# Experts' weights as two neighbouring rows per partition, all 1024 columns at once, a load's slot blocks in turn

## The chip, the cores and the metric

The kernel runs on one core of one Trainium2 chip. The metric is the device time of one execution in microseconds (us), the median over runs. The engines are TensorE (PE; its weight loads are listed apart as PEld), VectorE (DVE), ScalarE (ACT), GpSimd (POOL) and SyncE (SP), which here mainly issues DMAs.

## What is computed

The program is two transformer blocks, one after the other, all in float32. The first has four kinds of attention on 512 tokens. The second has two layers, each with attention, a convolution and a mixture of 16 experts in which every expert chooses its tokens. The change is in the experts of the second block and in the scale and shift that stand ahead of them:

```python
def ec_moe(h, w_router, w_gate, w_up, w_down):       # h: modulate(x, shift, scale)
    cap = EC_CAPACITY * n_tok // N_EXPERTS
    aff = softmax(einsum('bnd,de->bne', h, w_router))
    g, idx = lax.top_k(swapaxes(aff, 1, 2), cap)     # each expert takes cap tokens
    xs = vmap(lambda hb, ib: hb[ib])(h, idx)
    hid = silu(einsum('becd,edf->becf', xs, w_gate)) * einsum('becd,edf->becf', xs, w_up)
    ye = einsum('becf,efd->becd', hid, w_down) * g[..., None]
    return vmap(lambda yb, ib: zeros((n_tok, d)).at[ib.reshape(-1)].add(yb.reshape(-1, d)))(ye, idx)
```

An expert's gate, up and down matrices are 1024 x 1024 each, 4 MB. Layer 0 runs the experts on the latent tokens (64 per expert) and, with the same weights, on the context tokens (32 per expert). Layer 1 runs them on the latent tokens alone.

## The kernel before

`moe` (from L1103) goes through groups of experts: four groups of four in layer 0 (`two` is true), eight groups of two in layer 1. A group has blocks of up to 128 columns of gathered tokens. In layer 0 these are ctx (four experts of 32 tokens), lat0 and lat1 (two experts of 64 tokens each); in layer 1 it is one latent block. `gather` (L1150) fetches a block's token rows `r` with an indirect DMA on POOL's queue, transposes them on TensorE by pieces of 128 (`ptm`), and writes `xT` with scale and shift taken from the columns `modc`.

`wload` (L1126) brings 1 MB of one expert's matrix into a slot `w`: 512 contraction rows by 512 columns, where partition p holds rows p, 128 + p, 256 + p and 384 + p, so each run in memory is 512 columns, 2 KB. There are 14 slots in layer 0 and 18 in layer 1, filled in program order by SP's queue (the last few of the first turn of layer 1 by POOL's). The loads of the last group's down product are smaller in layer 1: 256 columns, runs of 1 KB.

`product` (L1190) multiplies one matrix, 512 columns at a time, with one PSUM bank (`pm`, six of them) for each block. Tokens are the stationary operand: experts of one block lie side by side in TensorE's columns (`tile_position`), four 32-wide or two 64-wide. In the order called `every`, each of the eight contraction steps k goes through ctx, lat0 and lat1 before the next k. Within a group, the loop at L1213 does gate and up for columns 0 to 511, then silu (ACT) into a tile `ty`, the product with up (DVE), and the transposes into `hid`; then the same for columns 512 to 1023. Down follows, again by two column halves. In all groups but the last of layer 0, `down` writes the weighted rows `ys`, and POOL adds them to `accc` (ctx) and `accl` (latent) in memory by indirect DMAs (L1334), one expert at a time. In layer 1, `spread` adds them instead by matmuls with a one-hot matrix `sel`. `r`, `ys` and, in layer 1, `xT` and `hid` are tiles of one pool, shown as `q`, of seven buffers.

`adaln` (L415) computes scale, shift and gates of a layer into `mr`, writes them to memory (`mod`), reads them back as `mraw` (L435), and transposes that to columns `modc`. It runs beside the attention; the second layer's begins by a MEMSET of its `mr` on POOL (L417) and four reads into it on SP (L419). The tile scheduler sets the order of instructions on an engine where the code's own order leaves it open; `pin` fixes some.

## Time and profile before

| | us |
|---|---|
| median of 3 runs | 2866.74 (2864.62 to 2875.64) |
| profiled execution, own time | 2861.59 |
| its span in the trace | 2859.8 |
| TensorE busy | 2483.4 (87%) |
| VectorE / ScalarE / POOL busy | 1228.3 (43%) / 802.2 (28%) / 504.6 (18%) |
| DMA | 612.94 MB, mean 214 GB/s |

The profiled execution lies 5.2 us below the median. TensorE's share of busy time is an average over stages with different limits, so the stages have to be read one by one. The experts of layer 0 take the stretch from 1300 to about 1937 us, those of layer 1 the stretch from about 2338 us to nearly the end. Matmuls in float32 are recorded twice each.

### The profile page before, as it was taken

How to read it: one execution, taken by the hardware profiler on the slowest of the kernel's cores; microseconds unless marked ns; L12 is line 12 of the kernel's file. 1: busy time of each engine (PE TensorE's matmuls, PEld its weight loads, DVE VectorE, ACT ScalarE, POOL GpSimd, SP SyncE). 2: the span in 40 equal slices, each digit the busy share in tenths (PEclk: the TensorE clock that was granted, in tenths of full speed). 3: DMA queues.
4: the chain of work that ended last, by engine and by line, in shares of the span. 5: the costliest groups of instructions: out<-in, count | busy, mean ns of one | idle time of the engine just before them, and what ended most of it. 6: DMA issues, size and time to landing. Idle time of an engine off the chain costs nothing.

```text
span 2859.8 us, 36332 instructions
## 1 busy us (share of the span) xinstructions
PE 2483.4 (87%) x14703; PEld 1412.3 (49%) x14703; DVE 1228.3 (43%) x2361; ACT 802.2 (28%) x1522; POOL 504.6 (18%) x389
## 2 busy tenths in 40 slices
PE   7988898998998878968999999995898869877886
PEld 5755676665687566753222222234677733323233
DVE  5423554335649968762010101028678641212113
ACT  3362323353335436521000000004247320000001
POOL 2111312012223332331010101004223320000001
PEclk9999999999999988988999999997999979999998
DMA  5364553346433141169999998963221479999997
GB/s 183 104 195 126 163 146 110 123 131 186 143 112 132 55 152 36 45 232 326 342 354 340 330 355 297 340 234 104 66 66 37 147 267 387 387 387 387 387 387 272
DMA packets 354191, 612.94 MB, mean 214 GB/s; under 512 B 37585, under 2 KB 110823, under 8 KB 354023
## 3 DMA queue, kind: packets, MB, share of 16 engines
q1 hardware_dynamic: 344214, 576.71, 58.4%
q0 software_dynamic: 5824, 20.45, 2.3%
q10 hardware_dynamic: 3984, 13.45, 1.2%
q8 instruction: 116, 1.90, 0.3%
q14 instruction: 53, 0.43, 0.0%
HBM read 581.88 MB, written 28.67 MB: 213 GB/s over the span
## 4 chain that ended last, share of the span: by engine, by line
PE 39%; DVE 11%; DMA 9%; issue 7%; ACT 3%; POOL 2%; SPq 0%; DVEq 0%; POOLq 0%; ACTq 0%
PE pm L151 24%; PE pj L151 6%; DMA w<-in_w_up_dram 5%; PE pa L151 5%; DMA w<-in_w_down_dram 3%; DVE acc L850 2%; PE pt L151 2%; PE pt L160 1%; DVE wl L331 1%; PE ptm L160 1%; POOL lnst L249 1%; DVE s L245 1%; ACT P L456 1%; DVE Q L1609 0%; DVE ng L453 0%
## 5 line engine op out<-in xcount | busy, mean ns | idle before, releaser
L151 PE MATMUL pm<-w,q 128*64 128x512 f32 (+1 forms) x1600 | 368.9, 583 | 56.2 <-DMA w<-in_w_up_dram 23.0
L151 PE MATMUL pm<-w,xT 128*64 128x512 f32 (+1 forms) x2048 | 389.4, 607 | 0.4 <-DVE xT L1168 0.3
L151 PEld LDWEIGHTS pm<-w,q 128*64 128x64 f32 x1600 | 124.8, 137 | 276.5 <-issue 174.7
L329 ACT ACTIVATE wh<-w 128x1024 fp32r<-128x1024 f32 (+2 forms) x154 | 161.0, 1050 | 303.4 <-PE pj L151 103.4
L1223 DVE TENSOR_TENSOR ty<-pm,ty 128x512 f32<-128x512 f32 x40 | 27.6, 691 | 502.9 <-PE pm L151 502.9
L151 PEld LDWEIGHTS pm<-w,xT 128*64 128x64 f32 (+1 forms) x2048 | 90.5, 123 | 281.1 <-issue 264.7
L151 PE MATMUL pj<-hTh,wh 128*128 128x512 f32 x512 | 214.4, 420 | 12.2 <-ACT ty L301 6.4
L331 POOL TENSOR_TENSOR wl<-w,wh 128x1024 fp32r<-128x1024 f32 (+1 forms) x57 | 142.4, 2500 | 436.6 <-ACT wh L329 403.9
L151 PE MATMUL pm<-w,hid 128*64 128x512 f32 (+1 forms) x1024 | 210.7, 604 | 0.0
L151 PE MATMUL pj<-hTl,wh 128*128 128x512 f32 x512 | 207.7, 406 | 0.0
L151 PE MATMUL pj<-hTh,wl 128*128 128x512 f32 x512 | 205.1, 404 | 0.0
L331 DVE TENSOR_TENSOR wl<-w,wh 128x1024 fp32r<-128x1024 f32 (+2 forms) x97 | 136.3, 1405 | 104.0 <-ACT wh L329 103.6
L160 PE MATMUL pt<-ident,P 128*128 128x128 f32 x712 | 120.5, 289 | 11.2 <-DVE mx L133 3.1
L151 PE MATMUL pa<-wh,hTh 128*128 128x512 f32 x256 | 106.2, 416 | 23.2 <-DVE ty L948 15.1
L151 PEld LDWEIGHTS pm<-w,hid 128*64 128x64 f32 (+1 forms) x1024 | 47.1, 122 | 154.6 <-issue 152.2
L151 PEld LDWEIGHTS pj<-hTh,wh 128*128 128x128 f32 x512 | 100.2, 196 | 38.9 <-issue 8.1
L1219 ACT ACTIVATE ty<-pm 128x512 f32<-128x512 f32 x40 | 23.9, 597 | 314.6 <-PE pm L151 314.6
L151 PEld LDWEIGHTS pj<-hTl,wh 128*128 128x128 f32 x512 | 99.8, 195 | 24.1 <-issue 3.9
L151 PEld LDWEIGHTS pj<-hTh,wl 128*128 128x128 f32 x512 | 98.7, 193 | 24.4 <-issue 2.2
L135 DVE TENSOR_SCALAR P<-P,rc 128x256 f32<-128x256 f32 (+6 forms) x176 | 107.8, 635 | 4.4
L453 DVE TENSOR_REDUCE ng<-pa 128x1 f32<-128x513 f32 (+5 forms) x124 | 93.3, 756 | 36.9 <-PE pa L151 35.0
L151 PE MATMUL pa<-wh,hTl 128*128 128x512 f32 x256 | 104.4, 412 | 1.1 <-DVE hTl L370 1.1
(441 smaller groups left out, 4332.7 us busy)
## 6 DMA issues: line engine op xcount, KB each, us to landing
w<-in_w_gate_dram SPq DMA_DIRECT2D x128, 1024.0 KB
w<-in_w_up_dram SPq DMA_DIRECT2D x127, 1024.0 KB
w<-in_w_down_dram SPq DMA_DIRECT2D x118, 1024.0 KB
w<-in_w_mod_dram SPq DMA_DIRECT2D x96, 512.0 KB
w<-in_w_in_dram SPq DMA_DIRECT2D x94, 512.0 KB
w<-in_w_out_dram SPq DMA_DIRECT2D x40, 512.0 KB
w<-in_w_down_dram SPq DMA_DIRECT2D x16, 512.0 KB
z<-q ACTq DMA_DIRECT2D x8, 512.0 KB
```

What stands on the lines that cost most here:

```text
L135: (G if eng == "g" else V).tensor_scalar(o, i, scale, None, op0=OP.mult)
L151: return T.matmul(o, l, r, start=start, stop=stop_, skip_group_check=True, **kw)
L160: T.transpose(o, i, ident[: i.shape[0], : i.shape[0]])
L245: pin(V.bn_stats(s6[:, c, :], x[:, c * w:c * w + w]))
L249: pin(G.tensor_tensor(out=rs, in0=ve, in1=mhalf[:, :n], op=OP.pow))
L329: A.activation(hi, w, AF.Copy)
L331: (lo_eng or (G if lot[0] % 3 == 0 else V)).tensor_tensor(out=lo, in0=w, in1=hi.bitcast(F32), op=OP.subtract)
L453: V.tensor_reduce(ng, S_[:, :, lo:hi], axis=AX, op=OP.max, negate=True)
L456: A.activation(P[:, i, lo:hi], S_[:, i, lo:hi], AF.Exp, bias=ng[:, i:i + 1], accum_out=su[:, i:i + 1])
L850: V.scalar_tensor_tensor(acc[:, c, :n], glu[:, c, tap:tap + n], w, acc[:, c, :n], op0=OP.mult, op1=OP.add)
L1219: A.activation(x, g, AF.Silu)
L1223: V.tensor_tensor(out=gs[bi], in0=u, in1=gs[bi], op=OP.mult)
```

## The change

Three things change together.

First, the layout of a load. `wwide` brings 512 rows by all 1024 columns in halves: partition p holds rows 4p + m and 4p + m + 1 of a 512-row half, whole and next to each other in memory, so that one run is 8 KB. A load is still 1 MB, and a matrix still four loads (j = 0 to 3) per expert. The contraction rows are thus permuted, and what multiplies them has to follow: transposes of gathered rows and of the gate/up result read every fourth column (`wide_rows`), and scale and shift come from a new table `modw`. For that, `adaln` reads two small pieces of `mod` back into `mr`, and adds eight transposes of four columns, a copy and two additions for each layer. The last group's down product keeps `wload` and its layout.

Second, the order of the products. `wide` does both column halves of all blocks with all six `pm` banks; for each load index j, it runs the latent blocks and then ctx, each with two contraction steps and two column halves. In the first gate of layer 0 the ctx block goes ahead for three of the four loads. Silu, the product with up and the transposes into `hid` come after both halves. In layer 0 the silu result is in a buffer of the pool `q` (`t4`) in place of `ty`.

Third, down of all groups but the last is one `wide` product, after which `down` and `spread` run for both halves.

```diff
--- before.py
+++ after.py
@@ -401,6 +401,7 @@
     z_d = [dr.tile([S, D], F32, name=f"z{l}") for l in range(NL)]
     mod_d = [dr.tile([2, 6 * D], F32, name=f"mod{l}") for l in range(NL)]
     modc = [con.tile([128, 96], F32, name=f"modc{l}") for l in range(NL)]
+    modw = [con.tile([128, 8, 4], F32, name=f"modw{l}") for l in range(NL)]
     cT = con.tile([128, 8, 32], F32, name="cT")
 
     def cond():
@@ -440,6 +441,20 @@
             for sc in (1, 4):
                 s0 = 48 * c + 8 * sc
                 V.tensor_scalar(modc[l][:, s0:s0 + 8], modc[l][:, s0:s0 + 8], 1.0, None, op0=OP.add)
+
+        mrow = mr[0:4, 0:8, :].rearrange("p a b -> p (a b)")
+        for c in range(2):
+            nc.sync.dma_start(mrow[2 * c:2 * c + 2, :], mod_d[l][c, 3 * D:5 * D].rearrange("(a d) -> a d", a=2))
+        p = pj()
+        for k in range(8):
+            tr(p[:, 4 * k:4 * k + 4], wide_rows(mrow, k))
+        V.tensor_copy(modw[l].rearrange("p k c -> p (k c)"), p[:, :32])
+        for c in range(2):
+            V.tensor_scalar(modw[l][:, :, 2 * c + 1], modw[l][:, :, 2 * c + 1], 1.0, None, op0=OP.add)
+
+    def wide_rows(x, k):
+
+        return x[:, 512 * (k // 4):512 * (k // 4) + 512].rearrange("p (j m) -> p m j", m=4)[:, k % 4, :]
 
     def mc(l, c, chunk, k):
         o_ = 48 * c + 8 * chunk + k
@@ -1121,16 +1136,27 @@
         def pm():
             return psm.tile([128, 512], F32, tag="m", name="pm", bufs=6)
 
-        def wload(src, e, c0, n, kh):
+        def wslot():
             turn[0] = (turn[0] + 1) % len(order_)
             pool = order_[turn[0]]
-            w = pool.tile([128, 4, 512], F32, tag="w", name="w", bufs=slots[id(pool)])
+            return pool.tile([128, 2048], F32, tag="w", name="w", bufs=slots[id(pool)])
+
+        def wload(src, e, c0, n, kh):
+
+            w = wslot().rearrange("p (k c) -> p k c", k=4)[:, :, :n]
+            loads[0] += 1
+            nc.sync.dma_start(w, src[l, e, 512 * kh:512 * kh + 512, c0:c0 + n].rearrange("(k p) c -> p k c", p=128))
+            return w
+
+        def wwide(src, e, j):
+
+            w = wslot().rearrange("p (k c) -> p k c", k=2)
 
             late = len(order_) - LATE[l] <= loads[0] < len(order_)
             loads[0] += 1
-            w = w[:, :, :n]
-            pin((nc.gpsimd if late else nc.sync).dma_start(w, src[l, e, 512 * kh:512 * kh + 512, c0:c0 + n].rearrange(
-                "(k p) c -> p k c", p=128)), late)
+            m = 2 * (j % 2)
+            pin((nc.gpsimd if late else nc.sync).dma_start(
+                w, src[l, e].rearrange("(h p m) c -> p h m c", h=2, m=4)[:, j // 2, m:m + 2, :]), late)
             return w
 
         gms = {}
@@ -1158,10 +1184,11 @@
             for kk in range(2):
                 p = ptm()
                 for k in range(4):
-                    tr(p[:, 128 * k:128 * k + 128], r[:, 512 * kk + 128 * k:512 * kk + 128 * k + 128])
+                    tr(p[:, 128 * k:128 * k + 128], wide_rows(r, 4 * kk + k))
                 for k in range(4):
                     k_ = 4 * kk + k
-                    o, i_, g, b = xT[:, k_, :], p[:, 128 * k:128 * k + 128], mc(l, s["c"], 4, k_), mc(l, s["c"], 3, k_)
+                    b, g = (modw[l][:, k_, 2 * s["c"] + j:2 * s["c"] + j + 1] for j in range(2))
+                    o, i_ = xT[:, k_, :], p[:, 128 * k:128 * k + 128]
                     if k % 2:
                         A.activation(o, i_, AF.Identity, bias=b, scale=g)
                     else:
@@ -1205,26 +1232,52 @@
                                    k == 0, k == 7, tile_position=(0, c0))
                 return outs
 
+            lats = [b for b, x in enumerate(blocks) if x[2] is lat]
+            rest_ = [b for b, x in enumerate(blocks) if x[2] is not lat]
+
+            def wide(src, lhs, early=False):
+
+                ws = {(e, j): wwide(src, e, j) for j in range(4) for e in exps}
+                outs = {}
+                for b in (rest_ + lats if early else lats + rest_):
+                    outs[b] = pm(), pm()
+                steps = [(b, j) for j in range(4) for b in lats + rest_]
+                if early:
+                    first = [(b, j) for j in range(3) for b in rest_]
+                    steps = first + [x for x in steps if x not in first]
+                for b, j in steps:
+                    for k in (2 * j, 2 * j + 1):
+                        for h in range(2):
+                            for e, c0, m in blocks[b][1]:
+                                mm(outs[b][h][c0:c0 + m, :], lhs[b][:, k, c0:c0 + m],
+                                   ws[e, j][:, k % 2, 512 * h:512 * h + 512], k == 0, k == 7, tile_position=(0, c0))
+                return outs
+
             all_k = range(8)
             every = [(list(range(len(blocks))), all_k)]
             one_by_one = [([b], all_k) for b in range(len(blocks))]
             hid = [mB.tile([128, 8, 128], F32, tag=f"hid{j}", name="hid", bufs=1) if two else
                    row4().rearrange("p (a b) -> p a b", b=128) for j in range(len(blocks))]
-            for half in range(2):
-                order = one_by_one if i == 0 and half == 0 else every
-                gp = product(a["w_gate_2"], (512 * half, 512), [b[0] for b in blocks], order)
-                gs = []
-                for g in gp:
-                    x = half_tile()
-                    A.activation(x, g, AF.Silu)
-                    gs.append(x)
-                up = product(a["w_up_2"], (512 * half, 512), [b[0] for b in blocks], order)
-                for bi, u in enumerate(up):
-                    V.tensor_tensor(out=gs[bi], in0=u, in1=gs[bi], op=OP.mult)
+            xTs = [b[0] for b in blocks]
+            gp = wide(a["w_gate_2"], xTs, two and i == 0)
+            gs = {}
+            for b in gp:
+                gs[b] = t4() if two else None
+                for h in range(2):
+                    x = gs[b][:, h, :] if two else half_tile()
+                    A.activation(x, gp[b][h], AF.Silu)
+                    gp[b] = gp[b][:h] + (x,) + gp[b][h + 1:]
+            up = wide(a["w_up_2"], xTs)
+            for b in up:
+                for h in range(2):
+                    x = gp[b][h]
+                    V.tensor_tensor(out=x, in0=up[b][h], in1=x, op=OP.mult)
                     p = ptm()
                     for k in range(4):
-                        tr(p[:, 128 * k:128 * k + 128], gs[bi][:, 128 * k:128 * k + 128])
-                    copy(hid[bi][:, 4 * half:4 * half + 4, :].rearrange("p a b -> p (a b)"), p)
+
+                        tr(p[:, 128 * k:128 * k + 128], x[:, 128 * k:128 * k + 128] if final else
+                           x.rearrange("p (j m) -> p m j", m=4)[:, k, :])
+                    copy(hid[b][:, 4 * h:4 * h + 4, :].rearrange("p a b -> p (a b)"), p)
 
             if i == 0:
                 late_rows()
@@ -1309,6 +1362,8 @@
                     self.seen.add(nm)
 
             waiting = None
+            if not final:
+                dw = wide(a["w_down_2"], hid)
             for c, n in ((0, 256), (256, 256), (512, 256), (768, 256)) if final and not two else ((0, 512), (512, 512)):
                 x = Columns(c, n)
                 if final and two:
@@ -1317,7 +1372,7 @@
                         lambda dp: x.down(1, dp), lambda dp: x.spread(0), ([2], range(4, 6)), lambda dp: x.spread(1),
                         ([2], range(6, 8)), lambda dp: x.down(2, dp), lambda dp: x.spread(2)])
                     continue
-                dp = product(a["w_down_2"], (c, n), hid, one_by_one if final else every)
+                dp = product(a["w_down_2"], (c, n), hid, one_by_one) if final else {b: dw[b][c // 512] for b in dw}
                 for bi in range(len(blocks)):
                     x.down(bi, dp)
                 if not final:
```

TensorE, layer 0, first group, around the end of the first gate product (`xT` are tokens of gate and up, `ty` the silu result, 32 and 64 the widths of ctx and lat). Before:

```order
L151 MATMUL pm<-w,xT 64x512 x25
L151 MATMUL pm<-w,xT 32x512 x32
L151 MATMUL pm<-w,xT 64x512 x32
L160 MATMUL ptm<-ident,ty 128x128 x8
L151 MATMUL pm<-w,xT 32x512 x4
L151 MATMUL pm<-w,xT 64x512 x4
L151 MATMUL pm<-w,xT 32x512 x4
L151 MATMUL pm<-w,xT 64x512 x3
L160 MATMUL ptm<-ident,ty 128x128 x4
```

After:

```order
L151 MATMUL pm<-w,xT 32x512 x8
L151 MATMUL pm<-w,xT 64x512 x64
L151 MATMUL pm<-w,xT 32x512 x16
L151 MATMUL pm<-w,xT 64x512 x21
L151 MATMUL pm<-w,xT 32x512 x16
L151 MATMUL pm<-w,xT 64x512 x11
```

After the first product the blocks alternate with every contraction step, 4 by 4; now they alternate with every load index, mostly 16 by 16.

TensorE, layer 0, between the down product of the first group and the gate product of the second (the three `q` are the gathered rows of ctx, lat0 and lat1). Before:

```order
L151 MATMUL pm<-w,hid 64x512 x4
L160 MATMUL ptm<-ident,q_11625 128x128 x8
L151 MATMUL pm<-w,xT 32x512 x12
L160 MATMUL ptm<-ident,q_11646 128x128 x4
L151 MATMUL pm<-w,xT 32x512 x6
L160 MATMUL ptm<-ident,q_11646 128x128 x4
L151 MATMUL pm<-w,xT 32x512 x7
L151 MATMUL pm<-w,xT 64x512 x5
L160 MATMUL ptm<-ident,q_11667 128x128 x4
```

After:

```order
L151 MATMUL pm<-w,hid 32x512 x16
L160 MATMUL ptm<-ident,q_11652 128x128 x8
L160 MATMUL ptm<-ident,q_11673 128x128 x8
L151 MATMUL pm<-w,xT 64x512 x19
L160 MATMUL ptm<-ident,q_11694 128x128 x8
L151 MATMUL pm<-w,xT 64x512 x21
L151 MATMUL pm<-w,xT 32x512 x16
```

The transposes of two blocks now stand in one row of 16, where matmuls lay between them; the gate product begins with the latent blocks.

SP, where `adaln` of the first layer reads back `mod` and that of the second layer begins. Before:

```order
L435 DMA mraw<-mod_114 96x128
L321 DMA w<-in_w_out_dram 128x2x512
L419 DMA mr<-in_b_mod_dram 2x12x128 x4
L321 DMA w<-in_w_out_dram 128x2x512 x3
L787 DMA q_2818<-z_112 128x1024
```

After:

```order
L436 DMA mraw<-mod_114 96x128
L447 DMA mr<-mod_114 2x1024 x2
L321 DMA w<-in_w_out_dram 128x2x512 x4
L802 DMA q_2820<-z_112 128x1024
L321 DMA w<-in_w_out_dram 128x2x512
L1519 DMA P<-in_k_natpad_dram 120x128
L321 DMA w<-in_w_out_dram 128x2x512
L1520 DMA natr<-P 7680x1x128
L321 DMA w<-in_w_out_dram 128x2x512
L420 DMA mr<-in_b_mod_dram 2x12x128 x4
L321 DMA w<-in_w_out_dram 128x2x512
L321 DMA w<-in_w_in_dram 128x4x260 x2
```

Two reads into `mr` are new, and the four reads of the second layer's `mr` moved from behind the first `w_out` load to ahead of the last one.

## Rows read from the trace of the kernel before

**Rows 1.** Page, 40 slices of 71.5 us: TensorE's busy tenths, GB/s moved.
```profile
PE   7988898998998878968999999995898869877886
...
GB/s 183 104 195 126 163 146 110 123 131 186 143 112 132 55 152 36 45 232 326 342 354 340 330 355 297 340 234 104 66 66 37 147 267 387 387 387 387 387 387 272
```

**Rows 2.** Windows: length, busy us of each engine, TensorE's clock, DMA share, GB/s.
```profile
1270.00:1280.00 10.00, 5.40 (x48) 3.42 (x48) 3.41 (x11) 4.16 (x6) 1.10 (x2) 0.66 1.04 408
1500.00:1600.00 100.00, 100.00 (x502) 23.32 (x500) 6.40 (x9) 3.58 (x6) 0.00 (x0) 1.00 0.94 341
2400.00:2500.00 100.00, 85.85 (x380) 33.12 (x379) 17.32 (x29) 7.09 (x13) 0.94 (x1) 1.00 1.04 387
2600.00:2700.00 100.00, 78.54 (x328) 27.42 (x327) 14.61 (x24) 6.49 (x12) 0.94 (x1) 1.00 1.04 387
2810.00:2820.00 10.00, 8.71 (x54) 4.38 (x54) 1.01 (x2) 0.60 (x1) 0.00 (x0) 1.00 1.10 349
2820.00:2830.00 10.00, 9.52 (x76) 6.11 (x76) 5.33 (x16) 0.83 (x2) 0.00 (x0) 1.00 1.08 355
```

**Rows 3.** Instruction groups of 1300:1900, TensorE: busy us, mean ns, idle before.
```profile
L151 PE MATMUL pm<-w,xT 128*64 128x512 f32 x1024 | 252.9, 603 | 0.1
L151 PE MATMUL pm<-w,xT 128*32 128x512 f32 x1024 | 151.3, 611 | 0.3 <-DVE xT L1168 0.3
```

**Rows 4.** Timeline of POOL's scatters, layer 0: start, us, instruction, idle before.
```profile
1445.80 1.40 POOL L1334 DMA_INDIRECT accc<-q,idxe  x1 [135.05 <-DVE q L1263]
...
1463.86 1.41 POOL L1334 DMA_INDIRECT accl<-q,idxe  x1 [1.07 <-DVE xT L1168]
...
1471.34 1.40 POOL L1334 DMA_INDIRECT accl<-q,idxe  x1 [2.35 <-DMA accl<-q,idxe]
...
1603.75 1.36 POOL L1334 DMA_INDIRECT accc<-q,idxe  x1 [127.19 <-DVE q L1263]
```

**Rows 5.** Instruction groups of 2310:2860, TensorE, layer 1.
```profile
L151 PE MATMUL pm<-w,q 128*64 128x512 f32 x1472 | 352.5, 601 | 54.5 <-DMA w<-in_w_up_dram 23.0 <-DVE q L1168 10.8 <-DMA w<-in_w_gate_dram 9.7
```

**Rows 6.** Chain of waits, 2350:2860: start, us, what.
```profile
2475.99 14.18 DMA w<-in_w_down_dram
...
2542.28 14.19 DMA w<-in_w_down_dram
```

**Rows 7.** Timeline of weight loads (PEld) before layer 0's width alternates.
```profile
1309.08 0.13 PEld L151 LDWEIGHTS pm<-w,xT 128*32 128x32 f32 x4 [0.30 <-issue]
1309.51 0.13 PEld L151 LDWEIGHTS pm<-w,xT 128*32 128x32 f32 x4 [0.30 <-issue]
...
1324.29 0.14 PEld L151 LDWEIGHTS pm<-w,xT 128*64 128x64 f32 x2 [0.28 <-issue]
1324.72 0.14 PEld L151 LDWEIGHTS pm<-w,xT 128*64 128x64 f32 x2 [0.29 <-issue]
```

**Rows 8.** Timeline of weight loads, one k step in the `every` order.
```profile
1543.46 0.16 PEld L151 LDWEIGHTS pm<-w,xT 128*32 128x32 f32 x8 [0.81 <-issue]
...
1546.32 0.16 PEld L151 LDWEIGHTS pm<-w,xT 128*32 128x32 f32 x8 [0.81 <-issue]
```

**Rows 9.** Timeline of TensorE, from the down product to the next group's gate.
```profile
1769.43 1.09 PE L160 MATMUL ptm<-ident,q 128*128 128x128 f32 x8
1772.19 1.09 PE L160 MATMUL ptm<-ident,q 128*128 128x128 f32 x8 [1.66 <-ACT xT L1166]
```

**Rows 10.** Instruction groups of 1300:1900, weight loads.
```profile
L160 PEld LDWEIGHTS ptm<-ident,q 128*128 128x128 f32 x89 | 9.5, 142 | 15.4 <-issue 8.6 <-ACT xT L1166 4.4 <-PE pm L151 2.4
```

**Rows 11.** Timeline of SP's queue near the read of `mraw`.
```profile
353.87 0.35 SPq L435 DMA_DIRECT2D mraw<-mod  x1
...
381.40 17.53 SPq L321 DMA_DIRECT2D w<-in_w_out_dram  x2
```

**Rows 12.** Timeline of weight loads, where TensorE takes `mraw`.
```profile
378.81 0.14 PEld L160 LDWEIGHTS pj<-ident,mraw 96*128 96x128 f32 x1
```

**Rows 13.** DMA queues in 1270:1280: packets, MB, share.
```profile
q10 hardware_dynamic: 401, 1.51, 37.1%
```

## The prediction

> **What bounds the kernel now.** I began with the slices of the page [rows 1]: TensorE is busy nearly everywhere, while the DMA engines move over 320 GB/s for long in two stretches only. Both are the expert layers, so I read these in windows [rows 2].
>
> Layer 0 of the experts runs from about 1300 to 1937 us. TensorE is busy for all of 1500:1600 and the DMA share is 0.94 at 341 GB/s: TensorE bounds it. The table of its instructions confirms this: the 64- and 32-wide gate/up matmuls have 0.1 and 0.3 us of idle ahead of them [rows 3]. The first scatters of two neighbouring groups start 158 us apart (1445.80, 1603.75) [rows 4], so a group of four experts takes 158 us, of which its 48 loads need about 48 × 2.71 = 130 us of DMA (2.71 us is 1 MB at 387 GB/s).
>
> Layer 1 runs from about 2338 to 2850 us. Here 2400:2500 and 2600:2700 show DMA at 387 GB/s and share 1.04, with TensorE at 86 and 79 of 100 us [rows 2]; its gate/up matmuls stood idle for 54.5 us, mostly for loads of `w` [rows 5], and the chain of waits holds steps of 14 us on such loads, the same one (`w_down`) 66 us apart [rows 6], which is the time of a group of two experts. DMA bounds it.
>
> **TensorE's passes in layer 0.** The weight loads show the rhythm. Alone, two 64-wide matmuls side by side start every 0.43 us (1324.29, 1324.72), and so do four 32-wide ones (1309.08, 1309.51) [rows 7]. I call this a pass. In the `every` order one k step has two passes each for ctx, lat0 and lat1, six in all, so 2.58 us; it takes 1543.46 to 1546.32 = 2.86 us [rows 8]. So going from 32-wide to 64-wide and back costs 0.285 us per pair. Counted along the two orders, the gate, up and down products of layer 0 have 350 changes of width before and 106 after, and 1266 passes before and 1208 after (each program matmul is recorded twice; broken-off passes at the borders of loads count whole; 1152 is the least). The saving is (350 − 106)/2 × 0.285 = 34.8 us and 58 × 0.43 = 24.9 us, together **60 us**. Check: 1266 × 0.43 + 175 × 0.285 = 594 us, and some 192 transposes of 0.136 us add 26 us: 620 of the 636 us that the layer takes. Bounds: 45 us, if a change now hidden in a pass break costs more after it, to 70 us.
>
> **Transposes between products.** Before, only one of three group starts has 16 transposes in a row, and TensorE then waits 1.66 us for the scaled copy `xT` [rows 9]; the others lie between matmuls. After, all three have 16 in a row: +2 × 1.66 = 3.3 us. Between up and down, `hid` is now built for both halves at once: I take 0.6 us for each of four groups, between nothing and 1.7: +2.4 us.
>
> **Strided transposes.** Their input is now read every fourth element. A row of eight takes 1.09 us, 0.136 us each [rows 9], and one weight load 142 ns [rows 10]; none in this trace reads with such a stride. Some 168 do in layer 0, where TensorE has no slack. Bounds: nothing, if the load keeps hiding under the matmul ahead, or one more load each, 168 × 0.142 = 24 us. I take **9 us**, nearer to nothing, since the load lies beside the matmul. Against this change speaks the Trainium skill, "SBUF — State Buffer", section "Specifications (TRN2)": lines are 16 bytes, and an access that moves on to a new line each time pays a penalty; a stride of four fp32 does just that. Taken as a doubled load it makes this term 24 us in place of 9; no row here shows which. In layer 1 the same transposes lie beside loads, where TensorE has 14 to 21 us of slack in 100 [rows 2]; without that cover they would cost up to 128 × 0.142 = 18 us.
>
> **The permuted scale and shift.** Each layer adds two small reads of `mod` on SP's queue behind `mraw`, eight 4-column transposes, a copy and two adds. The read of `mraw` is issued at 353.87 [rows 11] and TensorE takes it at 378.81 [rows 12], so the new reads have 25 us of cover. New is a wait: POOL's MEMSET of the second layer's `mr` now comes after those transposes, and SP's reads into `mr` after it; behind them on SP stand one `w_out` load (381.40 [rows 11]) and the next `w_in` loads, behind it on POOL the next split `wl`. Since SP gets there at about 379 us anyway, I price the wait at 0 to 3 us. With 16 transposes: **+2 us**, between 0 and 6.
>
> **Loads in layer 1.** Per DMA engine, 387 GB/s is 84.7 ns for a 2 KB packet, and the 1 KB loads of the last group (349 and 355, mean 352 [rows 2]) give 46.5 ns. So 1 KB more costs 38.2 ns, and an 8 KB packet takes 84.7 + 6 × 38.2 = 314 ns: 418 GB/s, or 2.508 us for 1 MB where it was 2.710. Between 1270 and 1280 us, where 1.51 MB went in 401 packets of some 4 KB [rows 13], the rate was 408 [rows 2], so larger packets do gain. 184 loads of 1 MB run in this layer, 18 of them ahead of it: 166 × 0.202 = **33.5 us**. Bounds: nothing if 387 is the limit, 37 us at 422 GB/s. TensorE's cover: its work per group is about 0.82 × 66 = 54 us, and 24 loads take 60 us after, so DMA still ends last. In layer 0 loads fall from 130 to 120 us per group, off the path.
>
> **The sum.** 2861.6 (profiled run) − 60 + 3.3 + 2.4 + 9 + 2 − 33.5 = 2784.8 us. The median of the runs is 5.1 us above the profiled one; with that, **2790 us**. Layer 0's share is −45 us, or 158 − 45/4 = 147 us per group.
>
> **Rivals.**
> *The rate stays at 387.* Packets of 8 KB bring nothing. Against it speaks the step from 352 to 387 from 1 to 2 KB and the 408; for it, that the share is already 1.04. Then 2790 + 33.5 = 2824 us. The Trainium skill, "DMA: Bandwidth & Descriptors", section "Where 436 GB/s comes from", has reads from HBM bound near 358 GB/s, whatever the packet; the 387 of this trace already stands above that.
> *The strided reads cost a whole load or more each.* By the bound above 2790 + 15 = 2805 us.
> *Layer 0's gain goes into a new wait.* All six `pm` banks belong to one matrix, and `gs` now takes its buffers from the seven that `r` and `ys` use, so the silu of lat1 needs the ctx scatters of the group before done. Their chain runs from 1445.80 to past 1471.34 with some 7.5 us from one to the next (1463.86, 1471.34) [rows 4]: about 33 us. The silu is due when lat1's gate ends, and a gate matrix has 96 passes × 0.43 = 41 us. The margin is 8 us; if the chain grows beyond it, TensorE waits in each of three groups. If all 45 us went so: 2835 us.
> *Slower: long packets land slower.* An 8 KB run goes to one partition by one engine; if a 1 MB load took 2.95 us (355 GB/s, the rate of the 1 KB loads [rows 2]), layer 1 loses 166 × 0.24 = 40 us and layer 0 turns DMA-bound: a group moves 158 us × 345 GB/s = 54.5 MB, 141 us at 387, and 141 + 48 × 0.24 = 152.5 us then, saving 4 × 5.5 = 22 us: 2867 + 40 + 3 − 22 = 2888 us. It decides from about 2.89 us per load on. Nothing in the trace points there.
>
> **How the numbers follow.** Forecast 0.63 (2790 us, own range 2772 to 2812); rate stays 0.12 (2824); strided reads 0.10 (2805); lost gain 0.10 (2835); slower 0.05 (2888). The range 2764 to 2836 takes in all but the last and the tails. About 0.5%, 14 us, is what a measurement of this kernel tells from no change. All cases but the last are faster by more than that, though a sum of two of them reaches no change: faster 0.90, same 0.05, slower 0.05.
>
> **What would show it.** Right: layer 1's windows near 418 GB/s at the same share, with less TensorE idle before `w`; in layer 0 passes 0.43 us apart with longer stretches of one width, TensorE never idle, first scatters about 147 us apart; 16 transposes in 2.2 us plus one short wait. Wrong: 387 GB/s in layer 1; transposes 0.2 us apart or more; TensorE in layer 0 waiting for ACT's silu behind POOL's scatters, or for loads of `w`; SP late with `w_out` or `w_in` near 380 us.

## The result

The changed kernel takes 2794.35 us (median of 4 runs, 2792.01 to 2797.08) where the kernel before took 2865.68 us (4 runs): a ratio of 0.9746 (95% interval 0.9719 to 0.9774). Five more runs beside another set of the kernel before gave 2790.95 us and 0.9739 (0.9725 to 0.9753). The forecast was 2790 us. The first profiled execution took 2796.16 us of its own time, 65.4 us less than that of before (2861.59 us).

The time can be cut at four points that both traces have: the first gate matmul of layer 0's experts, the end of its last down matmul, the first expert matmul of layer 1 and the end of its last one. Each kernel was traced twice; the second trace is in brackets. Times in us.

| stretch | before | after | difference of the first traces |
|---|---|---|---|
| start to experts of layer 0 | 1300.4 (1303.7) | 1314.1 (1306.3) | +13.7 |
| experts of layer 0 | 632.0 (632.0) | 592.2 (592.4) | −39.8 |
| between the two | 406.0 (406.0) | 399.0 (398.0) | −7.0 |
| experts of layer 1 | 500.1 (499.9) | 466.0 (467.4) | −34.1 |
| end | 21.3 (21.3) | 23.1 (23.1) | +1.8 |

The two expert stretches repeat within 1.4 us. The stretch ahead of them does not: the same kernel took 1314 and 1306 us for it.

The page of the kernel after, with the busy tenths of TensorE and the GB/s in 40 slices (of 70 us), to be held against [rows 1]:

```profile
PE   7988889988998987995999999996888959988887
...
GB/s 185 108 180 112 159 180 83 106 183 146 147 120 151 58 109 112 8 166 208 378 371 334 412 336 414 322 313 80 94 69 35 121 221 415 420 421 421 421 421 233
```

Layer 1's slices, 387 GB/s before, stand at 415 to 421. The windows (length, busy us of TensorE, its weight loads, VectorE, ScalarE and POOL, TensorE's clock, DMA share, GB/s) answer to [rows 2]:

```profile
1500.00:1600.00 100.00, 96.65 (x582) 30.89 (x578) 10.80 (x17) 4.64 (x9) 3.51 (x4) 1.00 1.01 419
1600.00:1700.00 100.00, 98.61 (x570) 32.46 (x572) 9.58 (x19) 9.43 (x20) 12.25 (x10) 0.98 0.93 357
2400.00:2500.00 100.00, 85.07 (x368) 31.55 (x366) 21.37 (x37) 8.74 (x17) 1.87 (x2) 0.95 1.01 421
2600.00:2700.00 100.00, 90.02 (x388) 31.70 (x389) 13.79 (x23) 6.46 (x12) 0.94 (x1) 0.94 1.01 421
```

In layer 0 TensorE is no longer without gaps (96.65 and 98.61 of 100 us): it idles 13.0 us in all there, where the kernel before idled 2.1 us, 1.66 of them the wait in [rows 9]. In layer 1 DMA is still full, at 421 GB/s. Where TensorE waits is told by the groups of instructions in layer 0 and by the first group of layer 1, which answer to [rows 3] and [rows 5] (busy us, mean ns, idle before and its releasers):

```profile
L151 PE MATMUL pm<-w,xT 128*64 128x512 f32 x1024 | 237.2, 602 | 0.0
...
L160 PE MATMUL ptm<-ident,q 128*128 128x128 f32 x185 | 32.3, 312 | 13.0 <-ACT xT L1193 11.8 <-DVE hid L133 1.2
...
L151 PE MATMUL pm<-w,q 128*64 128x512 f32 x1472 | 343.1, 614 | 40.6 <-DMA w<-in_w_up_dram 28.0 <-DVE q L1195 12.6
```

The gate and up matmuls of layer 0 never wait. The transposes do, 13.0 us in all, 11.8 of them for ScalarE's scaled copies `xT`. In layer 1 the idle ahead of the matmuls fell from 54.5 to 40.6 us.

The weight loads show the new rhythm, to be held against [rows 7] and [rows 8] (start, us, instruction, idle before):

```profile
1504.61 0.20 PEld L151 LDWEIGHTS pm<-w,xT 128*64 128x64 f32 x4 [0.84 <-ACT q L1268]
1505.09 0.14 PEld L151 LDWEIGHTS pm<-w,xT 128*64 128x64 f32 x2 [0.29 <-issue]
...
1511.62 0.16 PEld L151 LDWEIGHTS pm<-w,xT 128*32 128x32 f32 x8 [0.81 <-issue]
1512.08 0.13 PEld L151 LDWEIGHTS pm<-w,xT 128*32 128x32 f32 x4 [0.30 <-issue]
...
1515.19 0.20 PEld L151 LDWEIGHTS pm<-w,xT 128*64 128x64 f32 x4 [0.84 <-issue]
```

Sixteen passes of two 64-wide matmuls take 7.01 us (1504.61 to 1511.62), eight of four 32-wide ones 3.57 us. Passes are still 0.43 us, so 24 of them need 10.32 of the 10.58 us: one pair of width changes costs 0.26 us, and it now comes once in 24 passes instead of once in six or fewer. POOL's scatters give the period of a group, 158 us in [rows 4]:

```profile
1454.43 1.48 POOL L1389 DMA_INDIRECT accl<-q,idxe  x1 [41.43 <-DVE q L1316]
...
1477.13 1.32 POOL L1389 DMA_INDIRECT accc<-q,idxe  x1 [0.36 <-issue]
...
1598.09 1.46 POOL L1389 DMA_INDIRECT accl<-q,idxe  x1 [43.28 <-DVE q L1316]
...
1741.72 1.45 POOL L1389 DMA_INDIRECT accl<-q,idxe  x1 [43.29 <-DVE q L1316]
```

1454.43, 1598.09, 1741.72: 143.7 us. The chain of eight scatters issues its last at 1477.13, 23 us after the first, where it took 25.5 us before (1445.80 to 1471.34 in [rows 4]).

The border between two groups is where TensorE waits. Its timeline, VectorE's and ScalarE's there, to be held against [rows 9], and windows of 10 and of 2 us:

```profile
1452.14 1.23 PE L160 MATMUL ptm<-ident,q 128*128 128x128 f32 x8
1457.32 1.59 PE L160 MATMUL ptm<-ident,q 128*128 128x128 f32 x8 [3.95 <-ACT xT L1193]
1458.84 10.05 PE L151 MATMUL pm<-w,xT 128*64 128x512 f32 x38
...
1451.42 4.04 DVE L1316 SCALAR_TENSOR_TENSOR q<-pm,gat,gm 128x512 f32<-128x512 f32 x6 [37.21 <-PE pm L151]
1455.38 0.72 DVE L1195 TENSOR_SCALAR xT<-ptm,modw 128x128 f32<-128x128 f32 x2
...
1455.88 1.74 ACT L1193 ACTIVATE xT<-ptm,modw 128x128 f32<-128x128 f32 x4 [34.93 <-DVE xT L1195]
...
1450.00:1460.00 10.00, 6.05 (x44) 3.17 (x36) 6.68 (x14) 2.67 (x7) 2.84 (x2) 0.90 1.01 410
1460.00:1470.00 10.00, 10.00 (x46) 3.53 (x42) 0.69 (x2) 0.67 (x2) 2.72 (x2) 0.93 0.94 316
...
1458.00:1460.00 2.00, 2.00 (x9) 1.04 (x10) 1.25 (x4) 1.06 (x3) 0.00 (x0) 0.50 1.02 360
1460.00:1462.00 2.00, 2.00 (x8) 0.51 (x6) 0.31 (x1) 0.67 (x2) 0.00 (x0) 0.65 1.08 326
1462.00:1464.00 2.00, 2.00 (x12) 0.57 (x10) 0.00 (x0) 0.00 (x0) 1.41 (x1) 1.00 1.00 379
```

The transposes of the first block are done at 1453.4 us; those of the second start at 1457.32, after 3.95 us of idle. VectorE spends the time from 1451.42 to 1455.46 on six weighted copies of the down product (L1316), and only then makes its share of `xT`; ScalarE's share waits for that. Behind the idle TensorE is slow for a while: the second row of transposes takes 1.59 us where the first took 1.23, and the next 38 recorded matmuls take 10.05 us, where the same 38 take 8.80 us in a run below (latdown2) at a granted clock of 1.00. The windows show why: after standing idle, TensorE has a granted clock of 0.50 from 1458 to 1460 us, the lower of its two levels (1.2 and 2.4 GHz), and 1.00 again from 1462 us on. This slow stretch costs 0.36 + 1.25 = 1.6 us here, and 1.5 to 1.6 us at the other two borders.

### The profile page after: what moved, and what is told of

It reads as the page before. It is cut to its first block, busy times and chain, and to the rows that moved or that the text cites. A ratio compares the mean times of both kernels' runs of the same rounds, so it can differ in the third digit from the quotient of the medians.

```text
span 2794.4 us, 36391 instructions
## 1 busy us (share of the span) xinstructions
PE 2431.3 (87%) x14719; PEld 1441.9 (52%) x14719; DVE 1222.1 (44%) x2367; ACT 802.0 (29%) x1522; POOL 508.8 (18%) x389
## 4 chain that ended last, share of the span: by engine, by line
PE 34%; DVE 12%; DMA 10%; issue 8%; ACT 2%; POOL 2%; DVEq 0%; POOLq 0%; SPq 0%; ACTq 0%
PE pm L151 21%; DMA w<-in_w_up_dram 4%; PE pj L151 4%; PE pa L151 4%; DMA w<-in_w_gate_dram 4%; DVE acc L865 3%; PE pt L151 2%; DMA w<-in_w_down_dram 1%; PE pt L160 1%; DVE wl L331 1%; PE ptm L160 1%; DVE s L245 1%; POOL lnst L249 1%; ACT P L471 1%; DVE Q L1664 1%
## 5 line engine op out<-in xcount | busy, mean ns | idle before, releaser
L151 PE MATMUL pm<-w,q 128*64 128x512 f32 (+1 forms) x1600 | 358.3, 595 | 40.6 <-DMA w<-in_w_up_dram 28.0
L151 PE MATMUL pm<-w,xT 128*32 128x512 f32 (+1 forms) x2048 | 356.3, 603 | 0.0
L151 PEld LDWEIGHTS pm<-w,xT 128*32 128x32 f32 (+1 forms) x2048 | 104.4, 125 | 245.0 <-issue 237.9
L151 PE MATMUL pm<-w,hid 128*32 128x512 f32 (+1 forms) x1024 | 187.4, 597 | 0.0
L1274 DVE TENSOR_TENSOR q<-pm,q 128x512 f32<-128x512 f32 x24 | 16.6, 692 | 289.8 <-PE pm L151 289.8
L151 PE MATMUL pa<-wh,hTh 128*128 128x512 f32 x256 | 105.7, 414 | 23.1 <-DVE ty L963 15.1
L1274 DVE TENSOR_TENSOR ty<-pm,ty 128x512 f32<-128x512 f32 x16 | 11.1, 691 | 256.0 <-PE pm L151 256.0
L1180 POOL DMA_INDIRECT q<-rowsl,idx x16 | 15.4, 960 | 571.9 <-PE ptm L160 568.3
L151 PEld LDWEIGHTS pm<-w,hid 128*32 128x32 f32 (+1 forms) x1024 | 51.9, 123 | 120.1 <-issue 117.8
L865 DVE SCALAR_TENSOR_TENSOR acc<-glu,vec,acc 128x512 f32<-128x512 f32 x120 | 108.6, 946 | 0.1
```

The costliest lines, as they stand in the source:

```text
L151: return T.matmul(o, l, r, start=start, stop=stop_, skip_group_check=True, **kw)
L865: V.scalar_tensor_tensor(acc[:, c, :n], glu[:, c, tap:tap + n], w, acc[:, c, :n], op0=OP.mult, op1=OP.add)
L1180: pin(G.indirect_dma_start(out=r, out_offset=None, in_=s["rows"][:], in_offset=bass.IndirectOffsetOnAxis(ap=s["idx"][:, i:i + 1], axis=0)) ...
L1274: V.tensor_tensor(out=x, in0=up[b][h], in1=x, op=OP.mult)
```

## The experiments

Each edit is to the changed kernel unless said otherwise. The diffs show the lines that matter; "..." marks what is left out.

**Length of the runs.** Two kernels keep 1 MB loads and long stretches of one width, and cut the load differently. The first (runs2k):

```diff
-                w, src[l, e].rearrange("(h p m) c -> p h m c", h=2, m=4)[:, j // 2, m:m + 2, :]), late)
+                w, src[l, e].rearrange("(h p m) c -> p h m c", h=2, m=4)[:, j // 2, :, c0:c0 + 512]), late)
...
-                    for k in (2 * j, 2 * j + 1):
-                        for h in range(2):
+                    for k in range(4 * (j // 2), 4 * (j // 2) + 4):
+                        for h in (j % 2,):
```

> The changed kernel with its loads cut the other way: four neighbouring rows per partition, 512 columns of each, so runs of 2 KB instead of 8 KB; 1 MB per load, the rows' permutation and the runs of equal width on TensorE stay (103 changes of width in layer 0, against 107). If the length of the run sets the rate of the loads: layer 1 back at 387 GB/s and a group of two experts at 66 us, its stretch about 500 us instead of 466, layer 0 about as in the changed kernel (143.7 us per group), so 2794 + 33 = about 2827 us. If the gain of layer 1 came from the order of loads and products and not from the run: 2794 us and 420 GB/s.

The second (runs4k):

```diff
-                w, src[l, e].rearrange("(h p m) c -> p h m c", h=2, m=4)[:, j // 2, m:m + 2, :]), late)
+                w, src[l, e].rearrange("(h p q m) c -> p h m q c", h=2, q=2, m=2)[:, j // 2, j % 2, :, :]), late)
...
-                    for k in (2 * j, 2 * j + 1):
+                    for q in range(2):
+                        k = 4 * (j // 2) + j % 2 + 2 * q
```

> The changed kernel with two rows per partition that are not neighbours (4p and 4p + 2, or 4p + 1 and 4p + 3): runs of 4 KB, everything else alike. By a fixed cost per packet of some 8 ns: 407 GB/s, 2.58 us per load, layer 1 longer by 166 x 0.09 = 14 us, 2808 us. If everything from 4 KB on runs at the same limit: 420 GB/s and 2794 us.

Measured: runs2k 2814.46 us (ratio to the kernel before 0.9815, 0.9798 to 0.9832), runs4k 2851.47 us (0.9941, 0.9922 to 0.9960). The windows of layer 1, runs2k first, then runs4k, and one of runs4k in layer 0:

```profile
2400.00:2500.00 100.00, 78.77 (x320) 26.88 (x322) 11.47 (x20) 5.86 (x11) 0.94 (x1) 0.82 1.05 387
```

```profile
1360.00:1450.00 90.00, 89.61 (x530) 28.67 (x528) 6.12 (x9) 4.84 (x9) 1.90 (x2) 1.00 0.99 378
2400.00:2500.00 100.00, 87.01 (x378) 31.07 (x380) 16.65 (x30) 8.07 (x16) 1.91 (x2) 0.93 1.02 409
```

In layer 1 the run sets the rate: 387, 409 and 421 GB/s with 2, 4 and 8 KB, and the stretch took 502.4, 481.3 and 466.0 us. That half of the theory holds, to 3 us. Layer 0 went otherwise than either theory said: 572.3 us with 2 KB, 20 us less than with 8 KB, and 621.3 us with 4 KB. TensorE's longest waits in layer 0 say why in part (us in total, times, longest), runs2k, then runs4k:

```profile
PE ptm L160 <- ACT xT L1193: 4.8, 3, 1.6
PE pm L151 <- DMA w<-in_w_gate_dram: 4.7, 3, 2.0
```

```profile
PE pm L151 <- DMA w<-in_w_gate_dram: 18.5, 6, 6.4
PE ptm L160 <- ACT xT L1192: 11.9, 3, 4.0
```

In runs2k a load holds one column half, so the first half's banks are done a load earlier. VectorE's timeline at its first border shows what that does:

```profile
1437.12 2.07 DVE L1316 SCALAR_TENSOR_TENSOR q<-pm,gat,gm 128x512 f32<-128x512 f32 x3 [29.27 <-PE pm L151]
1440.60 0.75 DVE L1316 SCALAR_TENSOR_TENSOR q<-pm,gat,gm 128x512 f32<-128x512 f32 x1 [1.42 <-PE pm L151]
1444.04 0.75 DVE L1316 SCALAR_TENSOR_TENSOR q<-pm,gat,gm 128x512 f32<-128x512 f32 x1 [2.68 <-PE pm L151]
1447.70 0.75 DVE L1316 SCALAR_TENSOR_TENSOR q<-pm,gat,gm 128x512 f32<-128x512 f32 x1 [2.92 <-PE pm L151]
1448.37 0.80 DVE L1195 TENSOR_SCALAR xT<-ptm,modw 128x128 f32<-128x128 f32 x2
```

Five of the six copies of L1316 are made while the product still runs, and one (1447.70) stands ahead of `xT`: the waits for `xT` fall from 11.8 to 4.8 us. With 4.7 us of new waits for gate loads, TensorE idles 11.3 us in layer 0 instead of 13.0. The larger part is its passes. Counted in the traces (matmul records of one width that start together), runs2k has 1172 and the changed kernel 1208, mainly because fewer 64-wide matmuls stand alone in a pass (24 against 76): 36 × 0.43 = 15.5 us. The two together are 17 of the 20 us. In runs4k the border waits are those of the changed kernel, 18.5 us of waiting for gate loads come on top, and the granted clock over layer 0 is 0.96 instead of 0.99; in layer 0 it reaches 378 GB/s at share 0.99, in layer 1 409 at 1.02. Why its packets are slower in layer 0 is not settled: by rate alone the 2 KB kernel should have waited more.

**Order of the widths.** The 8 KB loads stay, the blocks alternate with every contraction step and half (every):

```diff
-                for b, j in steps:
-                    for k in (2 * j, 2 * j + 1):
-                        for h in range(2):
...
+                if not early:
+                    turns = [(b, k, h) for k in range(8) for h in range(2) for b in rest_ + lats]
+                for b, k, h in turns:
```

> The changed kernel with its 8 KB loads, but products of layer 0 (after the first gate) that go through ctx, lat0 and lat1 for every contraction step and column half: 331 changes of width instead of 107 and 24 passes more. If changes of width are what layer 0 gained from: 224/2 x 0.285 + 24 x 0.43 = 42 us slower in layer 0, a group at about 155 us, layer 1 as in the changed kernel, 2830 to 2838 us. If layer 0's gain is due to the loads (rate, fewer waits at borders of loads) and not to the order of widths: 2794 us.

Measured: 2822.48 us (0.9837, 0.9817 to 0.9857), below the 2830 to 2838 us that the theory of the widths asked for. TensorE's waits in layer 0 (us in total, times, longest):

```profile
PE pm L151 <- DMA w<-in_w_gate_dram: 4.9, 3, 2.8
PE ptm L160 <- DVE hid L133: 2.3, 7, 0.4
PE pm L151 <- DVE hid L133: 0.9, 3, 0.3
```

Layer 0 takes 619.7 us, 27.5 more than in the changed kernel, a group 153.2 us (scatters to `accc` begin at 1453.70 and 1606.94), and layer 1 465.5 us. The increase is smaller than 42 us for two reasons. The 3.95 us waits at the borders are gone, since the gate product begins with ctx again, whose rows are transposed first; with the new waits for gate loads and for `hid`, TensorE idles 8.2 us in layer 0 instead of 13.0, and the slow stretches, 3 × 1.6 us, are gone too. That makes 27.5 + 4.8 + 4.8 = 37 us for the order itself. And the order costs less than was expected: counted in the traces, it has 331 changes of width against 107, but 1219 passes against 1208, 11 more and not 24, which by the same prices is 112 × 0.285 + 11 × 0.43 = 37 us. The theory holds, and layer 0's gain is not the loads': with 8 KB loads and the blocks alternating at every step it is only 632.0 − 619.7 = 12 us, and this kernel still has 43 passes fewer than the kernel before (1262), worth 18 us.

**The border, first try.** The copies of L1316 in the order lat0, lat1, ctx (latdown):

```diff
             if not final:
                 dw = wide(a["w_down_2"], hid)
+                if two:
+                    for bi in lats + rest_:
+                        for h in range(2):
+                            Columns(512 * h, 512).down(bi, {bi: dw[bi][h]})
...
```

> The changed kernel with the six weighted copies after the down product of layer 0 (down, L1316 on VectorE) taken block by block, lat0 and lat1 first, ctx last, instead of ctx first. In the changed kernel TensorE idles 3.95 us at each of three group borders. Theory: VectorE's queue is held by the ctx copy, which waits for the product that ends last, and then runs all six copies (4.0 us) ahead of the scaled copies xT that TensorE waits for. Then only two copies are left at the end of the product: idle falls to 1.2 to 1.7 us, with less of a half-clock stretch behind it, 3 x 2.3 to 3 x 4 us, 2782 to 2787 us. If TensorE waits for the two transposition banks as such (as with 1.66 us before): idle stays near 4 us and 2794 us.

Measured: 2811.43 us (0.9804, 0.9788 to 0.9821), 17 us slower than the changed kernel. The wait changed its cause. TensorE at the border:

```profile
1459.82 1.95 PE L160 MATMUL ptm<-ident,q 128*128 128x128 f32 x8 [5.89 <-DMA q<-rowsc,idx]
1463.60 1.95 PE L160 MATMUL ptm<-ident,q 128*128 128x128 f32 x8 [1.84 <-DMA q<-rowsl,idx]
```

TensorE waits for gathered rows (`q<-rowsc`, `q<-rowsl`). With the copies earlier, the scheduler had put the first scatter ahead of the next group's gathers on POOL, and the queue is served in order: the gathers were issued at 1449.84 to 1452.43 instead of 1327.56 to 1412.07. The run doesn't test the theory.

**The border, second try.** The same with POOL's order held: the scatters are emitted after the next group's gathers, both pinned (latdown2).

```diff
-                loads[0] < 20)
+                loads[0] < 20 or two)
...
+            while late_adds:
+                late_adds.pop()()
...
-                    G.indirect_dma_start(out=s["acc"][:], in_=ys[bi][c0:c0 + m, :], in_offset=None,
+                    pin(G.indirect_dma_start(out=s["acc"][:], in_=y[c0:c0 + m, :], in_offset=None,
...
+            late_adds.append(adds)
```

> The changed kernel with the weighted copies after down taken lat0, lat1, ctx, and with POOL's queue held to the changed kernel's order (the gathers of the next group ahead of the scatters), which latdown had lost: there the gathers came behind a scatter and TensorE waited 5.9 and 1.8 us for gathered rows at each border. TensorE's and POOL's orders are now those of the changed kernel; only VectorE's differs. Theory (VectorE's six copies in a row hold the scaled copies): idle at the three borders falls from 3.95 to 1.2 to 1.7 us each, with a shorter half-clock stretch after it; 7 to 12 us less, 2782 to 2787 us. Rival (the two transposition banks set the wait): 3.95 us stays, 2794 us.

Measured: 2792.81 us (0.9735, 0.9712 to 0.9758), which can't be told from the changed kernel; layer 0 takes 595.1 us. Its border:

```profile
1453.28 1.23 PE L160 MATMUL ptm<-ident,q 128*128 128x128 f32 x8 [1.60 <-ACT xT L1194]
1454.54 8.80 PE L151 MATMUL pm<-w,xT 128*64 128x512 f32 x38
...
1470.79 4.56 PE L151 MATMUL pm<-w,xT 128*64 128x512 f32 x14 [2.85 <-DMA w<-in_w_gate_dram]
```

The wait for `xT` fell to 1.60 us at all three borders, as the theory of VectorE's queue had it. Behind the one shown, the 38 records take 8.80 us at a granted clock of 1.00, so nothing is lost there; behind the second one, also 1.6 us, the clock did fall (0.50 from 1600 to 1602 us). But 2.85 us at 1470.79, and 5.8 us in layer 0, are now waits for gate loads, and behind this one the granted clock is 0.53 from 1470 to 1472 us. In this trace the gain was given back to a wait that had been hidden behind the first. The trace is of the slowest of four executions (2785.04 to 2798.06 us), so how often it goes so is not shown.

**What makes those loads late.** latdown2 without the scatters (noscatter):

```diff
-            late_adds.append(adds)
```

> latdown2 without the scatters of layer 0 (the expert outputs of its first three groups are not added, so they are missing from the result). In latdown2 the wait for the scaled copies fell as expected, from 3.95 to 1.6 us at each border, and waits of up to 3 us for loads of the gate matrix took its place (5.8 us in layer 0). Theory: the scatters slow the loads that were issued at the border (338 GB/s in the 10 us after it, 421 elsewhere): without them no such wait, layer 0 at 583 to 588 us instead of 595. Rival: those loads are late because their slots come free late, whatever else moves: the waits stay, layer 0 at about 595 us.

Measured: one execution, 2786.76 us; layer 0 takes 580.8 us, 2 us less than the theory's range, and has no wait for a load. Windows over the border and the DMA queues in the first of them (packets, MB, share; q1 carries the loads, q0 the scatters), latdown2, then noscatter:

```profile
1450.00:1460.00 10.00, 8.38 (x50) 4.01 (x44) 4.35 (x10) 3.37 (x8) 4.08 (x3) 1.00 1.03 367
1460.00:1470.00 10.00, 7.94 (x34) 2.84 (x30) 1.64 (x4) 1.78 (x4) 2.72 (x2) 1.00 0.95 338
...
q1 hardware_dynamic: 427, 3.10, 74.7%
q0 software_dynamic: 169, 0.56, 28.2%
```

```profile
1450.00:1460.00 10.00, 8.38 (x43) 3.55 (x44) 3.20 (x9) 3.38 (x8) 0.00 (x0) 1.00 1.01 418
1460.00:1470.00 10.00, 10.00 (x48) 3.82 (x46) 1.64 (x4) 2.96 (x6) 0.94 (x1) 1.00 0.44 160
...
q1 hardware_dynamic: 571, 4.15, 100.3%
```

In the first 10 us after the border DMA moves 418 GB/s without the scatters and 367 with them, at the same share. The scatters hold 28.2% of the engines' time for 0.56 MB, and the loads get 3.10 MB through instead of 4.15. In the next 10 us noscatter's TensorE has no gap (10.00), latdown2's has 2.06 us. So the scatters slow the loads, as far as one trace of each can show it: in the totals noscatter's one execution lies within the spread of latdown2's four. The 14 us between the two traces in layer 0 are more than the 5.8 us of waits, since the granted clock also fell behind them; over layer 0 it is 0.98 in latdown2 and 1.00 in noscatter.

**The strided transposes.** Every transpose is read contiguously (contig):

```diff
-        return x[:, 512 * (k // 4):512 * (k // 4) + 512].rearrange("p (j m) -> p m j", m=4)[:, k % 4, :]
+        return x[:, 128 * k:128 * k + 128]
...
-                        tr(p[:, 128 * k:128 * k + 128], x[:, 128 * k:128 * k + 128] if final else
-                           x.rearrange("p (j m) -> p m j", m=4)[:, k, :])
+                        tr(p[:, 128 * k:128 * k + 128], x[:, 128 * k:128 * k + 128])
```

> The changed kernel with every transpose read contiguously in place of every fourth column, so that contraction rows meet the wrong weights; the order on every engine stays. Eight transposes take 1.16 us from first to next matmul in the changed kernel and took 1.02 before. Theory (18 ns each, most of the longer weight load hidden): 168 x 0.018 = 3 us less in layer 0, 2791 us. Rival (a whole weight load each, the price of a doubled load): 24 us less, 2770 us.

Measured: 2789.13 us (0.9739, 0.9718 to 0.9760), layer 0 588.6 us, 3.7 less. The weight loads of the transposes in layer 0 and one set of eight at the border, the changed kernel, then contig (columns as above):

```profile
L160 PEld LDWEIGHTS ptm<-ident,q 128*128 128x128 f32 x184 | 24.9, 202 | 35.5 <-issue 16.4 <-ACT xT L1193 12.4 <-PE pm L151 2.5
```

```profile
L160 PEld LDWEIGHTS ptm<-ident,q 128*128 128x128 f32 x185 | 21.2, 148 | 36.7 <-issue 16.4 <-ACT xT L1193 13.0 <-PE pm L151 2.5
...
1444.30 1.09 PE L160 MATMUL ptm<-ident,q 128*128 128x128 f32 x8
```

The strided weight load takes 202 ns against 148, and eight transposes 1.23 us (1452.14 above) against 1.09. Of 54 ns, 18 reach TensorE's path; the theory of 3 us holds, and the rival's 24 us is out.

**modw.** The lines of `adaln` that make it go, and `gather` takes `modc` again (nomodw):

```diff
-                    b, g = (modw[l][:, k_, 2 * s["c"] + j:2 * s["c"] + j + 1] for j in range(2))
+                    b, g = mc(l, s["c"], 3, k_), mc(l, s["c"], 4, k_)
```

> The changed kernel without modw: the two reads into mr, the eight small transposes and the additions of both layers are left out, and the gathered rows take the unpermuted columns modc, so scale and shift are those of other columns. In the changed kernel the experts of layer 0 begin at 1314 us, in the kernel before at 1300 us. Theory A (modw costs the predicted 2 us, the rest is where TensorE's clock falls in this execution): layer 0 begins at 1308 to 1315 us, total about 2790 us. Theory B (the new wait of POOL and SP behind modw delays the attention): it begins near 1301 us, total about 2781 us.

Measured: 2798.29 us (0.9761, 0.9744 to 0.9779), not faster than the changed kernel. The experts begin at 1304.9 us, and the stretch between the two expert layers takes 408.5 us. Theory B is out as a cost of the whole kernel. The begin lies between the ranges of both theories, so by itself it supports neither. A closer count does tell something, since the traces differ by up to 10 us before `modw`'s first instruction: from SP's first read of `mraw` to the experts it takes 946.5 and 946.8 us in the two traces of the kernel before and 947.3 us in nomodw, and 949.9 to 957.1 us in the ten traces of kernels with `modw`.

**Both kernels once more.**

> The kernel before once more, for its stages. In its first profiled execution the experts of layer 0 began at 1300 us; nine executions of kernels that share the changed kernel's code ahead of them began at 1305 to 1320 us. If that stretch only varies with where TensorE's clock falls: it begins at 1303 to 1315 us here, with layer 0 at 632 us and layer 1 at 500 us again. If the change itself lengthened it: 1300 us again.

> The changed kernel once more, for its stages and a closer interval: layer 0 at 592 us and layer 1 at 466 us again, the stretch ahead of the experts 1308 to 1320 us, total 2788 to 2798 us, ratio 0.973 to 0.977.

Measured: before_again 2864.62 us, its experts begin at 1303.7 us, in the range expected if that stretch only varies, layer 0 632.0 and layer 1 499.9 us. after_again 2790.95 us (0.9739, 0.9725 to 0.9753), its experts begin at 1306.3 us, 2 us ahead of the range expected, layer 0 592.4 and layer 1 467.4 us. In the kernels with `modw` the experts began at 1306 to 1320 us.

**A combination.** Layer 0 with column halves (2 KB runs, as in runs2k), layer 1 with 8 KB runs, and the order of latdown2 (mixdown2):

```diff
+            rows = src[l, e].rearrange("(h p m) c -> p h m c", h=2, m=4)[:, j // 2]
             pin((nc.gpsimd if late else nc.sync).dma_start(
-                w, src[l, e].rearrange("(h p m) c -> p h m c", h=2, m=4)[:, j // 2, m:m + 2, :]), late)
+                w, rows[:, :, c0:c0 + 512] if two else rows[:, m:m + 2, :]), late)
...
```

> A combination: layer 0 with loads of four rows by 512 columns (runs of 2 KB, as in runs2k, whose layer 0 took 572 us against 592), layer 1 with runs of 8 KB (466 us), and the weighted copies lat0, lat1, ctx with POOL's order held. If the two layers are independent and the column halves are what shortened layer 0: 565 to 572 us and 466 us, total 2768 to 2776 us. If layer 0 of runs2k was short because of something that its layer 1 or its own start gave it: layer 0 near 590 us, total 2794 us.

Measured: 2773.16 us, ratio 0.9674 (0.9656 to 0.9692), faster than both kernels. Layer 0 takes 572.6 us, layer 1 467.9 us. Since runs2k had 572.3 us without the new order of copies, that order adds nothing here; the column halves, with 1172 passes as in runs2k, do it.

## Why the prediction was right, and where it was not

*What bounds the kernel.* Right for both layers. Layer 1 stayed DMA-bound at 421 GB/s. Layer 0 stayed TensorE-bound, but with so little cover on the DMA side that a shorter wait at the border brings out a longer one for loads (latdown2, noscatter).

*Loads in layer 1, −33.5 us.* Right: −34.1 us in the first traces, −32.5 in the second ones. The extrapolation from 1 and 2 KB packets gave 407 GB/s for 4 KB and 418 for 8 KB; 409 and 421 were measured. The rivals of 387 GB/s and of slower landing (2.95 us a load) are out; 421 GB/s is 2.49 us a load. The Trainium skill, "DMA: Bandwidth & Descriptors", section "Where 436 GB/s comes from", has reads from HBM bound near 358 GB/s, half of what a stack gives its two cores. With one core at work no run here shows that bound: layer 1 ran at 387, 409 and 421 GB/s.

*Passes and widths, −60 us.* Right, as far as the parts can be separated. Counted in the traces, passes fell from 1262 to 1208 and changes of width from 351 to 107. The net change of layer 0 is −39.8 us. Against it stand 10.9 us more idle (13.0 against 2.1), 3 × 1.6 = 4.8 us of slow stretches behind the border waits and 3.7 us for the strided reads; without these it would be −59.2 us. The experiment on the order alone gives 37 us for its 224 changes and 11 passes, and the prediction's prices make 37.

*Transposes between products, +3.3 us.* This term failed. The prediction took the 1.66 us wait of [rows 9] for all that 16 transposes in a row cost, and multiplied it. It put at nothing what else VectorE has to do at that moment, and what the clock does after a wait; so its sign "TensorE never idle" didn't come. With all six banks finishing together and ctx last, six copies stand ahead of `xT` in VectorE's queue, the wait is 3.95 us at each of three borders, and the clock falls behind it: 3 × (3.95 + 1.6) − 1.66 = 15.0 us in place of 3.3. latdown2 confirms the cause: the wait is 1.60 us when the latent copies go first, close to the 1.66 us that the prediction had multiplied, so the rest of the 3.95 us is VectorE's queue. The waits for `hid` were 1.2 us, against 2.4.

*Strided transposes, +9 us.* Too large: 3.7 us. The rival of a whole load each is out. Going towards the low end was right, for the reason given: the longer load lies beside the matmul. The Trainium skill, "SBUF — State Buffer", section "Specifications (TRN2)", has a penalty for accesses that move to a new line each time; the load did grow, by 54 of 148 ns, so not to the double.

*modw, +2 us.* Its direct cost is about as priced: the eight small transposes take 1.12 us in each layer, and POOL's MEMSET of `mr` waits for them at 386.53 us without holding back the next split. The stretch ahead of the experts was 2.6 to 13.7 us longer than in the kernel before, the one between the layers 7 to 8 us shorter. The prediction had neither. The first stretch varies by 13 us between executions of kernels that share its code, but not all of its increase is chance: counted from the read of `mraw`, every trace with `modw` takes longer than each of the three without, by 2.6 to 10.6 us. Between the layers part of that comes back: 398.0 to 406.7 us with `modw`, 406.0, 406.0 and 408.5 us without. The two stretches together took +6.7 us in the first traces and −5.4 in the second ones, and nomodw was not faster, so no net cost is shown; by which path `modw` or the order that it brings shifts the time stays open.

*The sum.* −76.8 us was forecast; −65.4 (first traces), −75.7 (second ones) and, by the medians, −71.3 and −74.8 us were measured. That it came so close is in part luck. In layer 0 errors cancelled: 11.7 us too little for the border, against 5.3 too much for the strides and 1.2 too much for `hid`. And the stretches outside the two expert layers, for which the forecast had only +2 us, came to +8.5 us in the first traces and −3.6 in the second ones, the end's +1.8 us included.

*The rivals.* Layer 0's gain did not go into the scatters: their chain became no longer (last issue 23 us after the first, 25.5 before), and the silus waited for TensorE alone (117.1 us in layer 0). But the scatters matter in another way than the rival said, through the loads that run beside them (latdown2 against noscatter).

## What to carry to other kernels

A saving in a stage bound by one engine is worth what the borders of the stage leave of it: look at which queue each engine stands in when several results finish at once, and put first what ends first. When a wait is removed, look for what was hidden behind it before counting the gain, on the DMA side too. The layout that is best for the transfers of one layer need not be best for another: here 8 KB runs pay where DMA binds, and column halves pay where TensorE binds, through fewer passes that hold one matmul alone.

## What the runs showed of the hardware

Loads with runs of 1 KB (half a MB each) moved 352 GB/s, and loads of 1 MB with runs of 2, 4 and 8 KB 387, 409 and 421 GB/s; per DMA engine, a fixed cost of 8.3 ns a packet and 38.2 ns per KB describe all four within 1%. Beside accumulating scatters, which held 28.2% of the DMA engines' time for 0.56 MB in 10 us, the 8 KB loads moved 3.10 MB where they moved 4.15 MB without. A weight load that reads every fourth float took 202 ns instead of 148, of which 18 ns of the 54 more reached TensorE's path. Behind 3.95 us of idle TensorE was granted half its clock for a while and lost 1.6 us at each of three borders; behind 1.6 us of idle it kept a clock of 1.00 at the border shown and fell to 0.50 at the next one of the same trace (latdown2).
